# A hybrid decoder layer on one core: two feature groups interleaved in a written order, one more seven-product block, a last bank in two halves

## The chip, the cores and the metric

The kernel runs on one core of a Trainium2 chip. The metric is the device time of one execution in microseconds; a comparison takes the median of several. The engines are TensorE (PE, its weight loads PEld), VectorE (DVE), ScalarE (ACT), GpSimd (POOL) and SyncE (SP), which here issues the DMAs.

## The reference

One decoder layer for 256 tokens of width 2048, in fp32. What matters here is the first stage, the input projection, and the last, the layer norm of the output:

```python
def reference(x, mem, w_in, ...):
    proj = x @ w_in[l]
    q_m, k_m, v_m, o_m, i_m, f_m, q_a, k_a, v_a = split_columns(proj, IN_SPLITS)
    y_m = mlstm_mixer(q_m, k_m, v_m, o_m, i_m, f_m, conv_w[l], conv_b[l], gate_b[l], mh_g[l])
    y_a = dilated_attention(q_a, k_a, v_a, rel_bias)
    y = jnp.concatenate([y_m, y_a], axis=-1) @ w_out[l]
    x = layer_norm(DEEPNORM_ALPHA * x + y, ln_g[l, 0], ln_b[l, 0])
    y = memory_cross_attention(x, mem, xq[l], xk[l], xv[l], xo[l])
    x = layer_norm(DEEPNORM_ALPHA * x + y, ln_g[l, 1], ln_b[l, 1])
    y = swiglu_ffn(x, w1[l], w3[l], w2[l])
    x = layer_norm(DEEPNORM_ALPHA * x + y, ln_g[l, 2], ln_b[l, 2])

def mlstm_mixer(...):          # forget gates: log_sigmoid, cumulative sum, running maximum
    b = jnp.cumsum(log_f, axis=-1)
    m_row = jnp.maximum(inter, d_log.max(-1))
    ...

def dilated_pattern(q, k, v, rel_bias, window, dil):   # a bias table by distance, one row per head
    s = jnp.einsum('bhrnqd,bhrnkd->bhrnqk', qb, kc) * (dh ** -0.5) + bias[:, None, None]
    ...
```

## The kernel before

**Products.** Every fp32 product is made of parts: an operand is split into an upper part (a cast by ScalarE, name ending in h, L139 or L144) and a lower part (the rest, a subtraction on VectorE, name ending in l, L140 or L145), and upper × upper, upper × lower and lower × upper are summed in a bank of PSUM. x lies in eight pairs of k tiles (xT0 to xT7, L186 and L211), each 256 KB.

**Groups.** A *feature group* (i0 to i7) makes 512 columns of the query and key projections with the columns as rows of the result: eight tiles, each a k tile pair of weights, 128x1024, in 16 matmuls (eight pairs of one with 512 columns and one with 256) into four banks b0 to b3. A *row group* (v0, v1, v2 for the value columns) makes a 256 x 1024 result in four banks, named P2, P3, Q4 and E. Its plan (PLAN_V, L49) lists eight blocks of two k tiles each. A plain number is a block of 24 matmuls of 512 columns; a number in parentheses is a block by seven products (Strassen's scheme with fewer additions), 21 matmuls. For these, VectorE makes sums of the weights (L529, L537, L541), and the x of that block must have been mixed: `mix_again` (L182) adds the parts of x (L186), forms four sums of 128x128 (L175 to L178) and splits them again (ScalarE, then VectorE L140) into xTm.

**Order.** From the list `mix` on, the order of TensorE, VectorE and ScalarE is written by hand: `Stream(4)` (L407) goes through its tiles in the order in which they were added, makes the parts of the tile that is four ahead behind the products of the tile at hand (`upper` casts, `lower` subtracts), and hangs other work on a tile number at one of five places (0 ahead of the first products, 1 and 2 behind the first and second half, 3 ahead of the lower part, 4 behind it). Weights pass through 3 raw buffers (tag w, 1 MB each) and 5 buffers each for upper and lower parts. PSUM has a pool of five banks (`bank`) and one of three (`sbank`).

**The head.** i0 and i1 are made by `gemm_features` (L618) and `features` (L636) before the list begins: i0 whole, then i1 whole, in an order that the scheduler chooses. i0 loads x as it goes. The bias table (`bias_table`, L680) follows in the program: a small product pb of the one-hot table with rel_bias, a row in DRAM (line), a fetch of it broadcast over partitions (rows), and sixteen DMAs that cut it into the slots tb. Then come the constants of the convolution and gates (cw, gb, gw) and the mixes of x for j = 2, 4, 6. The list starts with v0, then i2, i3, the heads of the attention (scores sc, exponentials, `weigh` L739, and `turn` L747, which transposes on TensorE into pt), and the gates (`Gates`, L777): products, logarithms, a shift by a DMA (v0r, L812), the scans of sum and running maximum (L816 to L824, `maxima`), columns and exponents.

**The end.** The last row group is w2b1, with the products for its last eight k tiles and the second 128 rows kept back behind the list (`behind`, `kept`, LAG2 = 8). The loop at the end takes these products bank by bank, adds each to z (L1001), takes statistics (L1059), and then `finish` (L1070) scales the four pieces of z by mean and gain (L1077), then all four by the deviation (L1080), and four DMAs of 256 KB write them.

## Time and profile before

| | |
|---|---|
| median of 3 runs | 1525.39 us (1524.21 to 1526.31) |
| the profiled execution | 1525.3 us, span 1523.5 us |
| granted TensorE clock, mean | 0.998 |
| busy: PE, DVE, ACT | 1507.6, 1322.4, 832.9 us |
| DMA | 301.90 MB, 198 GB/s mean |

The span is the time from the first to the last instruction. Matmuls overlap: a matmul of 512 columns shows 0.39 us, but the next starts 0.23 us behind it, so stretches of TensorE are measured from start to start. In a timeline, x4 behind a row stands for four like instructions under one start. Where a row ends in brackets, its engine was idle before it for that long, and what stands behind the arrow ended the idle time.

### The profile page before, as it was taken

To read this page: it belongs to the slowest core of one execution; us is meant where nothing else is said; L and a number is where in the kernel's file an instruction comes from. 1 tells how busy PE (TensorE), PEld (TensorE's weight loads), DVE (VectorE), ACT (ScalarE), POOL (GpSimd) and SP (SyncE) were. 2 spreads that over 40 slices of the span, in tenths; PEclk is the share of its full clock that TensorE was granted. 3 is DMA by queue.
4 is the path that set the end of the run, shared out by engine and by line. 5 is a ranking of instruction groups with operands and counts; after the bars stand their busy time and mean duration, and the time that the engine had idled before them with its cause. 6 is when DMAs were issued, how large, how long until landed. Compare 5 with 4: busy or idle time off the path is not lost.

```text
span 1523.5 us, 19428 instructions
## 1 busy us (share of the span) xinstructions
PE 1507.6 (99%) x7340; PEld 1263.0 (83%) x7340; DVE 1322.4 (87%) x1756; ACT 832.9 (55%) x1089; POOL 8.9 (1%) x18
## 2 busy tenths in 40 slices
PE   9999999999999999999999999999999999999997
PEld 7888888888888888889888888888888888888885
DVE  7676699989999898777798889999998899998898
ACT  5455555545554456645556556556555555555551
POOL 0000000000000000000000000000000000000000
PEclk9999999999999999999999999999999999999999
DMA  8665446655656456454455465665565656666652
GB/s 306 227 231 187 165 157 224 219 196 208 202 213 221 166 196 218 166 204 156 155 181 201 161 214 194 194 208 182 196 228 180 216 194 198 198 201 222 235 194 111
DMA packets 82475, 301.90 MB, mean 198 GB/s; under 512 B 7133, under 2 KB 9422, under 8 KB 58318
## 3 DMA queue, kind: packets, MB, share of 16 engines
...
q8 instruction: 57, 0.93, 0.3%
...
## 4 chain that ended last, share of the span: by engine, by line
PE 95%; DVE 2%; issue 1%; DMA 1%; ACT 1%; SPq 0%; DVEq 0%; ACTq 0%
PE w2a0P L481 2%; PE w2a1P L481 2%; PE w2b1P L481 2%; PE w2b0P L481 2%; PE f8P L481 2%; PE f4P L481 2%; PE f10P L481 2%; PE f6P L481 2%; PE wo0P L481 2%; PE f14P L481 2%; PE f20P L481 2%; PE f18P L481 2%; PE f16P L481 2%; PE v1P L481 2%; PE f12P L481 2%; PE wo1P L481 2%
## 5 line engine op out<-in xcount | busy, mean ns | idle before, releaser
L144 ACT CAST w2a1h<-w2a1w 128x1024 fp32r<-128x1024 f32 (+1 forms) x24 | 22.7, 963 | 18.4 <-PE w2a1E L481 10.0
L145 DVE TENSOR_TENSOR w2a1l<-w2a1w,w2a1h 128x1024 fp32r<-128x1024 f32 (+1 forms) x24 | 25.8, 1107 | 3.0 <-ACT w2a1h L144 3.0
L144 ACT CAST w2a0h<-w2a0w 128x1024 fp32r<-128x1024 f32 (+1 forms) x24 | 22.5, 962 | 10.6 <-PE w2a0E L481 5.9
L145 DVE TENSOR_TENSOR v0l<-v0w,v0h 128x1024 fp32r<-128x1024 f32 (+1 forms) x16 | 17.7, 1121 | 11.3 <-ACT v0h L144 11.3
L481 PE MATMUL w2a0P<-w2a0h,hT 128*128 128x512 f32 x76 | 26.7, 392 | 0.0
L481 PE MATMUL w2a1P<-w2a1h,hT 128*128 128x512 f32 x76 | 26.5, 389 | 0.0
L145 DVE TENSOR_TENSOR w2a0l<-w2a0w,w2a0h 128x1024 fp32r<-128x1024 f32 (+1 forms) x24 | 26.0, 1106 | 0.4 <-ACT w2a0h L144 0.3
L144 ACT CAST w2b0h<-w2b0w 128x1024 fp32r<-128x1024 f32 (+1 forms) x20 | 19.5, 989 | 12.2 <-PE w2b0E L481 5.2
L145 DVE TENSOR_TENSOR w2b0l<-w2b0w,w2b0h 128x1024 fp32r<-128x1024 f32 (+1 forms) x20 | 22.2, 1137 | 3.9 <-ACT w2b0h L144 3.9
L145 DVE TENSOR_TENSOR xo0l<-xo0w,xo0h 128x1024 fp32r<-128x1024 f32 (+1 forms) x16 | 18.2, 1155 | 8.4 <-ACT xo0h L144 8.4
L294 PE MATMUL f0b<-f0h,x 128*128 128x512 f32 x64 | 25.4, 397 | 0.0
L295 PE MATMUL f0b<-f0l,x 128*128 128x512 f32 x64 | 25.1, 391 | 0.2 <-DVE f0l L1529 0.2
L144 ACT CAST w2b1h<-w2b1w 128x1024 fp32r<-128x1024 f32 (+1 forms) x20 | 18.7, 986 | 10.7 <-PE w2b0E L481 5.4
L603 PE MATMUL i2b<-xT,i2h 128*128 128x512 f32 x64 | 23.5, 408 | 0.5 <-DVE xTr L1159 0.5
L481 PE MATMUL w2b0P<-w2b0h,hT 128*128 128x512 f32 x68 | 23.9, 392 | 0.0
L144 ACT CAST v0h<-v0w 128x1024 fp32r<-128x1024 f32 (+1 forms) x16 | 15.3, 971 | 15.4 <-PE v0E L481 6.0
L144 ACT CAST f12h<-f12w 128x1024 fp32r<-128x1024 f32 (+1 forms) x16 | 15.3, 973 | 14.7 <-PE f12E L481 6.8
L603 PE MATMUL xq0b<-x,xq0h 128*128 128x512 f32 x64 | 23.1, 404 | 0.0
L603 PE MATMUL i3b<-xT,i3h 128*128 128x512 f32 x64 | 23.1, 404 | 0.0
L603 PE MATMUL i5b<-xT,i5h 128*128 128x512 f32 x64 | 23.1, 403 | 0.0
L603 PE MATMUL i4b<-xT,i4h 128*128 128x512 f32 x64 | 23.1, 403 | 0.0
L603 PE MATMUL i7b<-xT,i7h 128*128 128x512 f32 x64 | 23.1, 402 | 0.0
...
## 6 DMA issues: line engine op xcount, KB each, us to landing
...
```

The costliest lines, as they stand in the source:

```text
L144: SC.copy(hi, src)
L145: return lambda: V.tensor_tensor(out=lo, in0=src, in1=as_f32(hi), op=ALU.subtract)
L294: T.matmul(banks[m][c], xh, wh[:, cs], start=n == 0, stop=False)
L295: T.matmul(banks[m][c], xh, wl[:, cs], start=False, stop=False)
L481: T.matmul(self.of[to], lhsT, rhs, start=to not in self.begun, stop=end)
L603: T.matmul(b, wh[:, cs], self.op.both(kt), start=kt == 0, stop=end, skip_group_check=True)
```

## The change

- i0 and i1 become feature groups of the list. Their first two tiles alternate (i0 0, i1 0, i0 1, i1 1), then i0's tiles 2 to 7, then i1's. i0's first six k tiles and i1's first four are loaded each by a DMA of its own (512 KB) instead of two together (1 MB), the first one still in two halves of 256 KB. In the first tile of each group the products with upper parts precede, in each half of the weights, those with lower parts. Bank b0 of i1 comes from the pool of five, b1 to b3 from the pool of three.
- rel_bias, one-hot table and gate constants are fetched four tiles before i0's last; the mixes of x, now for j = 2, 4, 6 and 1, hang on the tiles 3 and 1 before i0's last, one behind it, and 5 before it; the table is made three tiles behind i0's last tile, in a bank of the pool of five.
- v0's plan has a fourth seven-product block and another order: 0, 3, (2), (4), 5, (6), (1), 7.
- The gates' maxima, columns and exponents come one tile later.
- At the end, bank E's products of the last three kept k tiles (CUT = 3) are made in halves of 256 columns, the second half into a bank E2 of its own. Adds and statistics follow by halves. The scalings by mean and deviation alternate, each piece's DMA follows at once, and the last piece is scaled and written in two halves. z's second 128 rows have their statistics in halves of 256 throughout this norm.

SP, from i0's second pair of weights on, before; xTraw is x, i0w and i1w are weights, rb, cw, gb and gw the constants:

```order
L277 DMA i0w_159<-in_w_qk 128x2048
L217 DMA xTraw_181<-in_xT 128x512
L217 DMA xTraw_206<-in_xT 128x512
L277 DMA i0w_211<-in_w_qk 128x2048
L217 DMA xTraw_233<-in_xT 128x512
L217 DMA xTraw_258<-in_xT 128x512
L217 DMA xTraw_285<-in_xT 128x512
L682 DMA rb<-in_rel_bias 32x8
L683 DMA rb<-in_one 1x8
L1135 DMA cw<-in_conv 128x80
L1137 DMA gb<-in_gate_b 8x1
L277 DMA i0w_263<-in_w_qk 128x2048
```

and after (xTd is a slot used first for the one-hot table, then for the last x):

```order
L217 DMA xTraw_190<-in_xT 128x512
L609 DMA i0w_164<-in_w_qk 128x1024
L217 DMA xTraw_216<-in_xT 128x512
L217 DMA xTraw_243<-in_xT 128x512
L217 DMA xTraw_269<-in_xT 128x512
L675 DMA rb<-in_rel_bias 32x8
L676 DMA rb<-in_one 1x8
L678 DMA xTd_282<-in_onehot 33x511
L1143 DMA cw<-in_conv 128x80
L1144 DMA gb<-in_gate_b 8x1
L1145 DMA gw<-in_w_gate 128x128
L609 DMA i0w_221<-in_w_qk 128x1024 x2
```

The small fetches, which stood ahead of i0's last pair only, stand ahead of its last two pairs, one of them in two loads; before these rows, SP now also issues two loads of i1 (rows not shown).

VectorE before, at i0's last two k tiles (i0l are lower parts of weights, xT of x; xTr is a mix being made):

```order
L177 TENSOR_TENSOR xTr_545<-xTr_545 128x128
L140 TENSOR_TENSOR xT_260<-xTraw_258,xT_260 128x2x256
L140 TENSOR_TENSOR xT_287<-xTraw_285,xT_287 128x2x256
L178 TENSOR_TENSOR xTr_545<-xTr_545 128x128
L186 TENSOR_TENSOR xTr_554<-xT_260 128x512
L140 TENSOR_TENSOR i0l_266<-i0w_263,i0h_265 128x1024
L175 TENSOR_TENSOR xTr_554<-xTr_554 128x128
L176 TENSOR_TENSOR xTr_554<-xTr_554 128x128
L140 TENSOR_TENSOR i0l_291<-i0w_263,i0h_290 128x1024
```

and after (xTm is the mixed x):

```order
L145 TENSOR_TENSOR i0l_276<-i0w_274,i0h_275 128x1024
L186 TENSOR_TENSOR xTr_280<-xT_126 128x512
L175 TENSOR_TENSOR xTr_280<-xTr_280 128x128
L176 TENSOR_TENSOR xTr_280<-xTr_280 128x128
L177 TENSOR_TENSOR xTr_280<-xTr_280 128x128
L178 TENSOR_TENSOR xTr_280<-xTr_280 128x128
L140 TENSOR_TENSOR xTm_287<-xTr_280,xTm_287 128x512
L140 TENSOR_TENSOR xT_315<-xTd_282,xT_315 128x2x256
L145 TENSOR_TENSOR i0l_319<-i0w_274,i0h_318 128x1024
```

Before, a mix was spread between other work; now the mix of x1, from L186 to its lower part (L140), and the last x stand in one piece between the lower parts of i0's k tiles 6 and 7.

VectorE before, at the end of i2 (v0r are the gates' rows, g and ast the softmax of a head, i3l lower parts):

```order
L145 TENSOR_TENSOR i3l_1090<-i3w_1087,i3h_1089 128x1024
L816 SCALAR_TENSOR_TENSOR xTr_563<-v0r_873,g_1029 4x256
L817 TENSOR_TENSOR xTr_563<-v0r_873,xTr_563 4x256
L818 SCALAR_TENSOR_TENSOR i0r_316<-xTr_563,g_1029 4x256
L824 TENSOR_TENSOR i0r_316<-xTr_563,i0r_316 4x256
L145 TENSOR_TENSOR i3l_1116<-i3w_1087,i3h_1115 128x1024
L741 RECIPROCAL ast_1093<-ast_1093 128x2
L743 TENSOR_SCALAR g_1030<-g_1030,ast_1093 128x256
L743 TENSOR_SCALAR g_1030<-g_1030,ast_1093 128x128
```

and after:

```order
L145 TENSOR_TENSOR i3l_1110<-i3w_1108,i3h_1109 128x1024
L145 TENSOR_TENSOR i3l_1137<-i3w_1108,i3h_1136 128x1024
L736 RECIPROCAL ast_1114<-ast_1114 128x2
L738 TENSOR_SCALAR g_1051<-g_1051,ast_1114 128x256
L738 TENSOR_SCALAR g_1051<-g_1051,ast_1114 128x128
L811 SCALAR_TENSOR_TENSOR tb_524<-v0r_894,g_1050 4x256
L812 TENSOR_TENSOR tb_524<-v0r_894,tb_524 4x256
L813 SCALAR_TENSOR_TENSOR xTd_459<-tb_524,g_1050 4x256
L819 TENSOR_TENSOR xTd_459<-tb_524,xTd_459 4x256
L145 TENSOR_TENSOR i3l_1161<-i3w_1159,i3h_1160 128x1024
```

The softmax (reciprocal and scaling, L741 and L743 before, L736 and L738 after) and the second lower part of i3 now precede the scans (L816 to L824 before, L811 to L819 after).

The diff, cut to what the prediction speaks of:

```diff
-MIXED_X = (2, 4, 6)
-PLAN_V = [[0, 1, (2,), 3, (4,), 5, (6,), 7]] * 3
+MIXED_X, MIX_X, BOTH, TABLE = (2, 4, 6, 1), (-3, -1, 1, -5), 2, 3
+PLAN_V = [[0, 3, (2,), (4,), 5, (6,), (1,), 7]] + [[0, 1, (2,), 3, (4,), 5, (6,), 7]] * 2
...
-        def __init__(self, stream, op, src, name, load=None, last=False):
-            self.name, self.rows, self.banks, self.t = name, [], [], {}
+        def __init__(self, stream, op, src, name, load=None, last=False, alone=0, own=4):
+            self.name, self.rows, self.banks, self.t, self.stream = name, [], [], {}, stream
             self.op, self.src, self.load, self.last, self.w = op, src, load, last, {}
+            self.alone, self.own = alone, own
             self.begin = len(stream.tiles)
-            for n in range(KT // 2):
-                parts = []
-                stream.tile(
-                    lambda n=n, parts=parts: self.prepare(n, parts), lambda n=n, parts=parts: self.products(n, parts)
-                )
-            self.end = len(stream.tiles) - 1
-            for j in range(2):
-                for c in range(2):
-                    stream.at(self.end, 2, self.evacuate, j, c)
+            if not alone:
+                for n in range(KT // 2):
+                    self.lay(n)
+
+        def lay(self, n):
+            parts = []
+            self.end = self.stream.tile(lambda: self.prepare(n, parts), lambda: self.products(n, parts))
+            if n == KT // 2 - 1:
+                for j in range(2):
+                    for c in range(2):
+                        self.stream.at(self.end, 2, self.evacuate, j, c)
 
         def prepare(self, n, parts):
             if self.load:
                 self.load(n)
-            if n % 2 == 0:
-                self.w[n // 2] = wp.tile([P, 2, W], F32, tag="w", name=f"{self.name}w{n // 2}", bufs=RAW)
-                nc.sync.dma_start(out=self.w[n // 2], in_=self.src[n // 2])
+            b, i = divmod(n, 2)
+            if i == 0:
+                self.w[b] = wp.tile([P, 2, W], F32, tag="w", name=f"{self.name}w{b}", bufs=RAW)
             parts += [wp.tile([P, W], F32R, tag=f"w{x}", name=f"{self.name}{x}{n}") for x in "hl"]
-            return upper_part(*parts, self.w[n // 2][:, n % 2])
+            w = self.w[b][:, i]
+            if self.alone and self.load and n == 0:
+                halves = [slice(c * 512, (c + 1) * 512) for c in range(2)]
+                for cs in halves:
+                    nc.sync.dma_start(out=w[:, cs], in_=self.src[b][:, i, cs])
+                for cs in halves:
+                    split(*(x[:, cs] for x in parts), w[:, cs])
+                return lambda: None
+            if n < self.alone:
+                nc.sync.dma_start(out=w, in_=self.src[b][:, i])
+            elif i == 0:
+                nc.sync.dma_start(out=self.w[b], in_=self.src[b])
+            return upper_part(*parts, w)
 
...
+    def bias_fetch():
         rb = const.tile([BUCKETS + 1, AH], F32, tag="rb", name="rb")
         nc.sync.dma_start(out=rb[:BUCKETS], in_=A["rel_bias"])
         nc.sync.dma_start(out=rb[BUCKETS:], in_=A["one"])
-        oh_t, gs_t = slot("oh"), slot("gs")
+        oh_t = slot("oh")
+        nc.sync.dma_start(out=oh_t[: BUCKETS + 1, :U], in_=A["onehot"])
+        table["rb"], table["oh"] = rb, oh_t
+
+    def bias_table():
+        rb, oh_t, gs_t = table["rb"], table["oh"], slot("gs")
         oh, gs = oh_t[: BUCKETS + 1, :U], gs_t[:AH, :U]
-        nc.sync.dma_start(out=oh, in_=A["onehot"])
-        pb = sbank("pb")
+        pb = bank("pb")
...
-                (0, 0, self.products), (1, 3, self.logs), (2, 4, self.shift), (4, 3, self.maxima),
-                (6, 0, self.columns),
+                (0, 0, self.products), (1, 3, self.logs), (2, 4, self.shift), (5, 3, self.maxima),
+                (7, 0, self.columns),
             ):
                 mix.at(t + dt, where, f)
             for h in range(MH):
-                mix.at(t + 8 + h, 3, self.exponents, h)
+                mix.at(t + 9 + h, 3, self.exponents, h)
...
+        def stats(self, m, c, halves=range(2)):
+            if m not in self.fine:
+                V.bn_stats(out=self.st[m][:, c], in_=z[m][c])
+                return
+            for i in halves:
+                V.bn_stats(out=self.st[m][:, 2 * c + i], in_=z[m][c][:, i * 256 : (i + 1) * 256])
...
+    i0 = FeatureGroup(mix, xT, A["w_qk"][0], "i0", load_x, alone=6)
+    i1 = FeatureGroup(mix, xT, A["w_qk"][1], "i1", alone=4, own=1)
+    for n in range(BOTH):
+        i0.lay(n)
+        i1.lay(n)
+    for group in (i0, i1):
+        for n in range(BOTH, KT // 2):
+            group.lay(n)
+    for t, j in zip(MIX_X, MIXED_X):
+        mix.at(i0.end + t, 4, xT.mix_again, j)
+    mix.at(i0.end - 4, 0, bias_fetch)
+    mix.at(i0.end - 4, 0, fetch_constants)
+    mix.at(i0.end + 1, 3, gate_weights)
+    mix.at(i0.end + TABLE, 2, bias_table)
     v0 = rows_group(0, PLAN_V[0], va)
     i2, i3 = features_group(2), features_group(3)
-    heads(0, lambda j: (qk0[j], qk0[2 + j]), 0, [i2.begin + ATT + 4 * h for h in range(4)])
...
+    def last_step(ln, scale, c, n):
+
+        for i in range(n):
+            cs = slice(i * 512 // n, (i + 1) * 512 // n)
+            t = z[1][c][:, cs]
+            V.scalar_tensor_tensor(out=t, in0=t, scalar=scale, in1=ln.b[c][:, cs], op0=ALU.mult, op1=ALU.add)
+            nc.sync.dma_start(out=A["out"][1, c][:, cs], in_=t)
+
+    for c in range(2):
+        add(0, 1, banks, 1.0, (c,))
+        ln.stats(0, 2 + c)
+    ln.finish(0)
+    for c in range(4):
+        nc.sync.dma_start(out=A["out"][0, c], in_=z[0][c])
+    for f in final.behind:
+        f(0)
+    add(1, 1, banks, 1.0, (0,))
+    ln.stats(1, 2)
+
+    final.of["E2"] = sbank("w2b1E2")
+    for f in final.behind[:-CUT]:
+        f(1)
+    for i in range(2):
+        cs = slice(i * 256, (i + 1) * 256)
+        for f in final.behind[-CUT:]:
+            f(1, cs)
+        t = z[1][3][:, cs]
+        for x in ("E", "E2")[: 1 + i]:
+            V.tensor_tensor(out=t, in0=t, in1=final.of[x][:, cs], op=ALU.add)
+        ln.stats(1, 3, (i,))
+    mean, scale = ln.scales(1)
+    t = z[1]
+    for c in range(4):
+        V.scalar_tensor_tensor(out=t[c], in0=t[c], scalar=mean, in1=ln.g[c], op0=ALU.subtract, op1=ALU.mult)
+        if c:
+            last_step(ln, scale, c - 1, 1)
+    last_step(ln, scale, 3, 2)
```

## Rows read from the trace of the kernel before

**Rows 1.** The page: busy time, share of the span and instructions of each engine.

```profile
PE 1507.6 (99%) x7340; PEld 1263.0 (83%) x7340; DVE 1322.4 (87%) x1756; ACT 832.9 (55%) x1089; POOL 8.9 (1%) x18
```

**Rows 2.** TensorE's waits: line, what for; us in total, times, longest.

```profile
PE i0b L628 <- ACT i0h L139: 1.4, 2, 1.1
PE pt L749 <- DVE g L743: 0.8, 1, 0.8
PE i2b L603 <- DVE xTr L1159: 0.5, 1, 0.5
```

**Rows 3.** Timeline of TensorE, head: start, duration, what [idle before <- releaser].

```profile
5.51 1.20 PE L628 MATMUL i0b<-xT,i0h 128*128 128x512 f32 x4 [0.27 <-ACT i0h L139]
9.78 1.20 PE L628 MATMUL i0b<-xT,i0h 128*128 128x512 f32 x4 [1.09 <-ACT i0h L139]
...
49.73 0.40 PE L628 MATMUL i1b<-xT,i1h 128*128 128x512 f32 x1
52.50 0.40 PE L628 MATMUL i1b<-xT,i1h 128*128 128x512 f32 x1
```

**Rows 4.** Windows: busy us (instructions) of PE, PEld, DVE, ACT, POOL, clock, DMA.

```profile
10.00:20.00 10.00, 9.58 (x51) 7.60 (x51) 9.86 (x17) 7.37 (x11) 0.00 (x0) 1.00 0.97 366
20.00:30.00 10.00, 10.00 (x59) 8.75 (x59) 10.00 (x18) 6.09 (x8) 0.00 (x0) 1.00 0.82 309
40.00:50.00 10.00, 10.00 (x60) 8.77 (x59) 6.62 (x6) 4.83 (x5) 0.00 (x0) 1.00 0.78 274
```

**Rows 5.** Timeline of SP: issue of two DMAs.

```profile
11.90 0.28 SPq L683 DMA_DIRECT2D rb<-in_one  x1
...
81.55 0.36 SPq L229 DMA_DIRECT2D v0w<-in_w_v  x1
```

**Rows 6.** Timeline of ScalarE: casts of i0's weights.

```profile
8.68 1.04 ACT L139 CAST i0h<-i0w 128x1024 fp32r<-128x1024 f32 x1 [1.03 <-DMA i0w<-in_w_qk]
...
11.91 2.00 ACT L139 CAST i0h<-i0w 128x1024 fp32r<-128x1024 f32 x2 [1.66 <-DMA i0w<-in_w_qk]
...
20.91 2.00 ACT L139 CAST i0h<-i0w 128x1024 fp32r<-128x1024 f32 x2 [1.60 <-DMA i0w<-in_w_qk]
```

**Rows 7.** Timeline of TensorE: start of v0, and eight spacings.

```profile
53.99 0.50 PE L481 MATMUL v0P<-v0h,xT 128*128 128x512 f32 x1 [0.53 <-DVE i0r L644]
...
59.11 0.39 PE L481 MATMUL v0P<-v0h,xT 128*128 128x512 f32 x1
...
60.92 0.39 PE L481 MATMUL v0E<-v0h,xT 128*128 128x512 f32 x1
```

**Rows 8.** Timeline of VectorE: first and last operation of a seven-product block.

```profile
79.53 1.22 DVE L529 TENSOR_TENSOR v0t<-v0w 128x1024 f32<-128x1024 f32 x1
...
84.89 1.22 DVE L145 TENSOR_TENSOR v0l<-v0s,v0h 128x1024 fp32r<-128x1024 f32 x1
```

**Rows 9.** Timeline of ScalarE: the cast of v0's last weights.

```profile
87.56 2.00 ACT L144 CAST v0h<-v0w 128x1024 fp32r<-128x1024 f32 x2 [2.71 <-DMA v0w<-in_w_v]
```

**Rows 10.** Timeline of TensorE: first and third pair of i2.

```profile
96.90 0.47 PE L603 MATMUL i2b<-xT,i2h 128*128 128x512 f32 x1
...
98.53 0.50 PE L603 MATMUL i2b<-xT,i2h 128*128 128x512 f32 x1
```

**Rows 11.** Timeline of VectorE: the gates' first scan.

```profile
119.94 0.68 DVE L816 TENSOR_TENSOR_SCAN xTr<-v0r,g 4x256 f32<-4x256 f32 x1 [2.45 <-DMA v0r<-v0r]
```

**Rows 12.** Chain that ended last, tail: start, us, what.

```profile
1513.34 0.70 DVE z L1001
...
1514.06 0.71 DVE l2st L1059
...
1514.79 0.27 DVE l2mv L1064
```

**Rows 13.** Groups of VectorE by form: statistics of 256 columns: busy, mean ns.

```profile
L942 DVE BATCH_NORM_STATS2 mst<-mh 128x6 f32<-128x256 f32 x8 | 3.0, 418 | 0.0
```

**Rows 14.** DMA issues of the tail: KB each, median us to landing.

```profile
out<-z SPq DMA_DIRECT2D x8, 256.0 KB, 2.0
```

123 lines of the change are left out of this document (45 added, 78 removed).

## The prediction

> **What bounds the kernel now.** I read the page first: TensorE is busy for 1507.6 us, 99% of the 1523.5 us span, and VectorE for 87% [rows 1]. So time can come from three places only: fewer products, waits of TensorE, and the ends of the span where it has nothing to do. The list of TensorE's waits comes next [rows 2]: the first feature group i0 waits 1.4 us for ScalarE's casts, one transposition (pt) waits 0.8 us and group i2 waits 0.5 us, all for work that the change moves. These sums are idle time only; what a stall costs is read from start to start in the timeline. In the head the first product starts at 5.51 and the second tile at 9.78, where TensorE waited 1.09 us for the cast of i0's second k tile; at the other end eight product pairs, one tile, take 52.50 − 49.73 = 2.77 us [rows 3]. Sixteen tiles of i0 and i1 are 44.3 us, and the first pair of the next group would start at 52.50 + 0.35 = 52.85. Hence 52.85 − 5.51 − 44.3 = 3.0 us were lost in the two groups, almost all of it in i0's first tiles. The windows say why: from 10 to 20 us the DMA engines are 0.97 busy and move 366 GB/s, and VectorE is busy for 9.86 of 10 us, then all of the next 10; from 40 to 50 it is down to 6.62 and TensorE is never short [rows 4]. The head waits for bytes, and next to that for VectorE.
>
> The sum below is made against the profiled run, 1525.3 us with a span of 1523.5 us. It lies 0.1 us below the median of the three runs, so I use it for the median too.
>
> **The first two groups side by side.** Today every tile of i0 needs a new 256 KB of x and, for each k tile, 512 KB of weights. With i1's first two k tiles put between, the second tile uses x that is already there. Its price: 1 MB of i1 is now fetched ahead of i0's later weights.
> - Second tile. Today its 512 KB are behind the second x and land just before the cast at 8.68 [rows 6]; now they are ahead of that x, 256 KB less. At the 366 GB/s of [rows 4] 256 KB are 0.7 us, so the cast starts near 7.9 and the tile near 9.0 instead of 9.78. TensorE is through the first tile at 5.51 + 2.77 + 0.3 (the wait for the second half of the first weights, which stays) = 8.6. Lost: 0.3 + 0.4, and 0.25 more for the lower part, which VectorE makes behind the cast. The third and fourth tiles bring one weight load each and one x between them, so they should find their data.
> - i0's last weights. SP issues a small DMA at 11.90 [rows 5], just as i0's second pair has landed for the cast at 11.91 [rows 6]: it waits for a landing, so the queue has a limited number in flight, and the six small fetches (bias, gate weights) now stand ahead of i0's k tiles 4 to 7, which is where the changed order costs. Today the last 1 MB of i0 lands just before the cast at 20.91 [rows 6]. One more MB ahead of it is 1.05 / 366 = 2.9 us: 23.7 us; with one or two more for the small fetches, and the one-hot table that today is fetched much later, 25.4. k tile 6 is the ninth tile and is due at 5.51 + 8 × 2.77 + 0.95 = 28.6, its cast (half of the 2.00 us for two, [rows 6]) and lower part (1.22, [rows 8]) in time. But VectorE has in its order, between the lower parts of k tiles 6 and 7, the whole first mix (two operations of 128x512 at about 0.7 and four of 128x128, an estimate of 0.27 each: 256 columns are 0.418 [rows 13], 512 are 0.71 [rows 12], so half of the 256 is 0.15 less), a cast of ScalarE inside it and the last x. From 25.4: cast 1.0, lower part 1.2, mix 0.7 + 1.1, cast 0.5, two of 0.65, lower part 1.1, that is 32.3. Tile 7 is due at 31.4. So I book a new wait of 0.9 there; from 23.7 it would be none.
> - Later tiles. A mix comes every second tile: two lower parts (2 × 1.15), a mix with its waits (some 2.9) are 5.2 us against 2 × 2.77 = 5.54 of TensorE. It fits, barely; I book 0.15.
> Lost after: 0.3 + 0.4 + 0.25 + 0.9 + 0.15 = 2.0, against 3.0: 1.0 gained, between 0 (a wait of 1.9 at tile 7) and 1.9.
>
> **The start of v0.** Its third product waited for the evacuation of i1 and started at 53.99, where spacing asks for some 53.3: 0.7 with what follows it [rows 7]. Now i1 ends in three banks of the small pool and one of the large, and v0 begins in banks that i0 left ten tiles earlier. Gain 0.7 to 0.8; I take 0.8. The bias table's product (pb) stands on TensorE in i1 as it did in v0, with the same operands: its time only moves, which I book at nothing.
>
> **One more seven-product block in v0.** Three products of 512 columns fewer. Eight spacings are 60.92 − 59.11 = 1.81 [rows 7], so each is 0.226 and the gain 0.68. It costs VectorE: a seven runs from 79.53 to the end of the lower part at 84.89 + 1.22, about 6.5 us [rows 8], against 21 × 0.226 = 4.75 us of TensorE. Two of these in a row fall 3.5 us behind; the plain blocks on either side (2.3 us of lower parts in 24 × 0.226 = 5.4) give 3.1 back each, and in [rows 4] VectorE has a third of its time free just ahead of this region. The cover is four tiles of work ahead. If it were gone, up to 1.7 us per seven would show, which is where the lower end of the range comes from. I book nothing. The new mix of x for it lies in the head and is booked above.
>
> **From v0 to i2.** The first pair of i2 starts at 96.90, the third at 98.53 [rows 10], where two pairs are 2 × 0.35 = 0.7: 0.9 lost, of which 0.5 is plain waiting [rows 2] for the sums that clear v0's banks. They are late because ScalarE waited 2.71 us for v0's last weights [rows 9], and these because their DMA was issued at 81.55 [rows 5], behind the sixteen table DMAs. Now the table is made in i1, some 17 us earlier, and two loads of v0 instead of one stand behind its DMAs. SP passes them long before. The sums then start earlier by up to the 2.5 us that VectorE idled, but four other steps and i2's lower parts stand ahead of them. Between 0 (the wait only moves) and 1.2 (the next pairs late by a third as well), I take 0.8.
>
> **Gates.** VectorE waits 2.45 us for the shifting DMA at 119.94 [rows 11], and the softmax that pt waits for is queued behind it. With the scans one tile (2.77 us) later, the softmax is ahead of them and the DMA has landed. TensorE's 0.78 [rows 2] costs 0.93 from start to start. Behind the scans now stand only the third lower part of i3, four tiles ahead, and the columns, moved by one tile as well. I take 0.93, between 0.5 and 0.95.
>
> **The tail.** TensorE pays nothing for eighteen products of 256 columns in place of nine of 512 but a few fixed costs, 0.05. VectorE after the last product: today add, statistics and aggregate start at 1513.34, 1514.06 and 1514.79 [rows 12]. Now the first half is ready 9 × 0.113 = 1.0 us before the end, at 1512.3, and three adds and two statistics of 256 columns follow; nearest row, 0.418 each [rows 13], 0.44 with the gap: 1512.3 + 2.2 = 1514.5. Gain 0.3. The last scaling is halved: the last DMA begins on 128 KB, and of the 2.0 us of a 256 KB one [rows 14] some 0.3 are bytes at 366 GB/s; against it stands one more fixed cost of VectorE, 0.15. Together 0.45, between 0.2 and 0.7. The halved statistics earlier in the group cost VectorE 2 × 0.418 for 0.71 [rows 12, 13], some 0.14 each; they run beside kept tiles, and I book 0.05 for all of them.
>
> **Sum.** 1.0 + 0.8 + 0.68 + 0.8 + 0.93 + 0.45 − 0.1 = 4.6 us: 1525.3 − 4.6 = 1520.7.
>
> **Rivals.**
> *The waits only move.* The sums of v0 come as late as before since VectorE makes i2's lower parts first, and the scans, now a tile later, hold up the columns instead. Then 0.8 + 0.93 fall away: gain 2.9, 1522.4, within 0.2% by a hair. For it: VectorE is 87% busy, and both waits are for VectorE. Against it: both have a DMA behind them in the rows, and the change passes these.
> *The bytes come late.* In the head 7.3 MB (x, i0 and the first MB of i1) must land before k tile 6. From about 2 us at 366 GB/s that is done at 22; if the six small transfers take places among the few in flight and cut the rate to 270 GB/s, it is 29.2, and tile 7, 6.9 us of cast, mix and lower parts later, is ready at 36.1, 4.7 us late where 0.9 is booked: gain 0.8, 1524.5. For it: the queue is bound by what is in flight [rows 5], and 309 GB/s is all that the next window shows [rows 4]. Against: that window is one in which SP waited for buffers.
> *Slower.* The same place with small loads as such: eight loads of 512 KB take the place of four of 1 MB. Slower by 3.05 us needs tile 7 to be 4.6 + 3.05 = 7.65 us later than booked: weights landed at 31.4 + 0.9 + 7.65 − 6.9 = 33.1, or a rate below 7.3 / (33.1 − 2) = 235 GB/s. Then 1528.4 or more. Against it stand 366 GB/s in a stretch that is half 256 KB loads of x, since several are in flight. The Trainium skill, "DMA: Bandwidth & Descriptors", section "Bandwidth", asks for 1 MB or more per DMA, and its "Anatomy of one DMA" gives about 2 us fixed plus bytes at 436 GB/s, by which (an estimate) one 512 KB load after the other would run at some 160 GB/s and this rival would hold with a time over 1535; the 366 GB/s show that the fixed part overlaps here.
> *Not what it says.* If the table's product, one tile earlier or later, met its own late fetch, TensorE would wait in i1; its fetch goes out ahead of i0's fifth k tile and is used some 20 us later, so I give this nothing.
>
> **How the numbers follow.** Forecast as summed: 0.72. Waits only move: 0.12. Bytes late: 0.11. Slower: 0.05. The upper ends of the terms together (1.9 + 0.8 + 0.68 + 1.2 + 0.95 + 0.7) are 6.2, 1519.1; the forecast's own range is 1519.1 to 1522.3. A measurement of this kernel tells 0.2%, 3.05 us, from no change: faster means below 1522.3. The first rival lies at that line; I count a fifth of it and a tenth of the second to faster: 0.75. Same: 0.20. Slower: 0.05. For 8 in 10 the range takes in the first rival and the easier part of the second, and 0.3 below the forecast's own for the scatter of a median: 1518.8 to 1523.3.
>
> **What would show it.** Right: the second tile near 9.0 and v0's first product near 52.9 with pb (about 1 us) already done; no wait of v0 for the evacuation; pt and i2 gone from TensorE's list; 21 products in each of four blocks of v0; aggregate about 1.2 us after the last product ends. Wrong: a wait of i0 or i1 for weights at 25 to 35 us, waits of v0 for VectorE's lower parts in the two adjoining sevens, or i2 still waiting for the sums.

## The result and the profile after

The changed kernel takes 1528.17 us (median of 19 runs, 1526.53 to 1530.40); the kernel before, run beside it, 1525.66 us (19 runs, 1524.21 to 1527.16). The ratio is 1.0016, with a 95% interval of 1.0010 to 1.0023. The forecast was 1520.7 us, in a range that ended at 1523.3: wrong in size and in sign. By the prediction's own bound of 0.2% the change made no difference that counts, but the interval lies above 1: 2.5 us were lost where 4.6 were to be gained.

The profiled execution of after took 1527.06 us with a span of 1525.2, against 1525.3 and 1523.5 before. It is one of the shorter ones of after, 1.1 us below the median, so that part of the loss stands in no trace of after. The page's line of busy times, which answers to [rows 1]:

```profile
PE 1508.5 (99%) x7346; PEld 1264.7 (83%) x7346; DVE 1330.4 (87%) x1774; ACT 835.5 (55%) x1092; POOL 8.9 (1%) x18
```

TensorE's waits, which answer to [rows 2] (us in total, times, longest):

```profile
PE i0b L624 <- ACT i0h L139: 2.6, 1, 2.6
...
PE i2b L624 <- DVE i1r L1158: 1.0, 1, 1.0
PE i0b L626 <- DVE i0l L145: 0.5, 1, 0.5
```

The wait of pt is gone. i0 has one wait of 2.6 us, i2 waits twice as long as before, and i0 waits for VectorE at its last k tile, where before it did so at its third (0.4 us, not in [rows 2]). Cut at the first product of a stage, the span divides like this (us; all starts are those of TensorE's instructions, "end" is the end of the span):

| stretch | before | after | difference |
|---|---|---|---|
| start to i0's first product | 5.51 | 5.29 | −0.22 |
| i0 and i1, to v0's first (after holds pb, 1.05) | 47.34 | 52.02 | +4.68 |
| v0, to i2's first (before holds pb) | 44.05 | 42.19 | −1.86 |
| i2, to i3's first | 32.22 | 31.71 | −0.51 |
| i3 to the last group, unchanged | 1331.60 | 1330.96 | −0.64 |
| last group, to its last product | 52.19 | 52.53 | +0.34 |
| last product to the end | 10.61 | 10.55 | −0.06 |

The unchanged stretch took between 1330.8 and 1331.9 us in fourteen profiles, so a sum of stages carries about 1 us of scatter, which the prediction had no row for. The loss sits in the second line. The next view is ScalarE's timeline in the head of after, the counterpart of [rows 6]:

```profile
9.26 0.62 ACT L139 CAST i0h<-i0w 128x512 fp32r<-128x512 f32 x1 [4.02 <-DMA i0w<-in_w_qk]
```

The second half of i0's first weights, 256 KB, was cast at 9.26; it had been issued at about 1.65, as in before. TensorE's timeline in the same place, the counterpart of [rows 3]:

```profile
9.93 2.08 PE L624 MATMUL i0b<-xT,i0h 128*128 128x512 f32 x4 [2.60 <-ACT i0h L139]
...
12.65 1.24 PE L624 MATMUL i1b<-xT,i1h 128*128 128x512 f32 x4
```

After 2.6 us without work, the four pairs from 9.93 took 2.72 us, where a half tile takes 1.39. The windows of after say why (columns as in [rows 4]):

```profile
4.00:6.00 2.00, 1.95 (x4) 0.62 (x3) 1.39 (x2) 0.81 (x2) 0.00 (x0) 1.00 0.74 152
6.00:8.00 2.00, 1.33 (x8) 1.00 (x6) 0.00 (x0) 0.00 (x0) 0.00 (x0) 1.00 0.85 246
8.00:10.00 2.00, 0.07 (x1) 0.07 (x1) 0.09 (x1) 0.62 (x1) 0.00 (x0) 0.89 1.01 406
10.00:12.00 2.00, 2.00 (x5) 1.62 (x6) 0.97 (x2) 1.45 (x2) 0.00 (x0) 0.50 1.04 418
...
16.00:18.00 2.00, 2.00 (x13) 1.72 (x13) 1.87 (x3) 1.35 (x2) 0.00 (x0) 1.00 0.57 193
18.00:20.00 2.00, 2.00 (x13) 1.76 (x12) 1.55 (x3) 1.57 (x2) 0.00 (x0) 1.00 0.28 91
```

And the same first windows of before:

```profile
4.00:6.00 2.00, 1.73 (x4) 0.45 (x3) 1.20 (x2) 0.72 (x2) 0.00 (x0) 1.00 0.91 224
6.00:8.00 2.00, 2.00 (x12) 1.67 (x11) 1.18 (x3) 1.24 (x2) 0.00 (x0) 1.00 1.05 386
8.00:10.00 2.00, 0.91 (x6) 0.66 (x6) 0.61 (x2) 1.32 (x2) 0.00 (x0) 1.00 1.05 434
```

Between 4 and 8 us the DMA engines moved 152 and 246 GB/s where they had moved 224 and 386. From 8 to 16 us the rates are alike; from 16 to 20 they fall to 193 and 91, where before had 209 and 407. The granted clock fell to 0.50, the 1.2 GHz level, while products ran, after the 2.6 us of idle.

Per tile (from one tile's first product to the next one's), with 2.77 as the prediction's measure:

```
before  4.27  3.24  3.54  then 2.66 to 3.01, mean 2.79
after   7.37  2.92  then 2.80 to 2.83 in ten tiles, 3.60 at the tile from 35.37, 3.82 with pb, 2.96 behind it, 3.10 the last
```

So once the first tile is through, TensorE waits only once more in the two groups. But that tile costs 4.6 us instead of 1.5, and the tile from 35.37 another 0.8. A tile in the steady part takes 2.83 rather than 2.79. That is not the change's doing: the head of before, in "the head undone", has 2.77 to 2.84 as well, after's order in the runs "xq" and "x early" has 2.77, and "three sevens" goes from 2.83 to 2.77 and back within the head, all at a granted clock of 1.00. What makes it 2.77 or 2.83 no run shows.

### The profile page after: what moved, and what is told of

The parts are those of the page before. It is cut to its first block, busy times and chain, and to the rows that moved or that the text cites. A ratio compares the mean times of both kernels' runs of the same rounds, so it can differ in the third digit from the quotient of the medians.

```text
span 1525.2 us, 19461 instructions
## 1 busy us (share of the span) xinstructions
PE 1508.5 (99%) x7346; PEld 1264.7 (83%) x7346; DVE 1330.4 (87%) x1774; ACT 835.5 (55%) x1092; POOL 8.9 (1%) x18
## 4 chain that ended last, share of the span: by engine, by line
PE 91%; DMA 3%; DVE 3%; issue 1%; ACT 1%; SPq 0%; DVEq 0%; ACTq 0%
PE w2a0P L482 2%; PE w2a1P L482 2%; PE w2b1P L482 2%; PE w2b0P L482 2%; PE f18P L482 2%; PE f4P L482 2%; PE f6P L482 2%; PE f16P L482 2%; PE wo0P L482 2%; PE f20P L482 2%; PE f14P L482 2%; PE f10P L482 2%; PE f8P L482 2%; PE v1P L482 2%; PE f12P L482 2%; PE wo1P L482 2%
## 5 line engine op out<-in xcount | busy, mean ns | idle before, releaser
L624 PE MATMUL i0b<-xT,i0h 128*128 128x512 f32 x64 | 23.6, 424 | 2.6 <-ACT i0h L139 2.6
L294 PE MATMUL f0b<-f0h,x 128*128 128x512 f32 x64 | 25.4, 397 | 0.0
L624 PE MATMUL i6b<-xT,i6h 128*128 128x512 f32 x64 | 23.2, 404 | 0.0
```

The lines of the kernel that those rows point to most:

```text
L294: T.matmul(banks[m][c], xh, wh[:, cs], start=n == 0, stop=False)
L624: T.matmul(b, w, self.op.both(kt), start=kt == 0, stop=end, skip_group_check=True)
```

## The experiments

Two theories stood against each other at first. A: the loss is the head's first tile, where i1's weights, as the fourth DMA, hold up the second half of i0's. B: it is VectorE, which a fourth mix and a fourth seven-product block overload. Times are medians; each ratio is against runs of before on the same chip. Each kernel has one profile, and a profile is one execution: that of "tail undone" is 1.3 us above its median, that of "i0 first" 1.4 below.

**The head undone.** Everything of the change but the first two groups, which run as before: one after the other, 1 MB loads, table in v0.

```diff
-    for n in range(BOTH):
-        i0.lay(n)
-        i1.lay(n)
...
+    qk0 = in_features(0, load_x) + in_features(1)
+    tb = bias_table()
```

> The change with i0 and i1 made as before it (one after the other, 1 MB loads, order of the scheduler, table and constants as before); v0's fourth seven, the gates and the tail stay as changed. Theory A (the loss is in the head: the second half of i0's first weights lands at 9.2 instead of 6.3 us, TensorE waits 2.6 us and then runs at the lower clock): the first tile is on time again, v0 starts about 2.5 us earlier counted without pb, and the time is about 1525.7 us. Theory B (the loss is in v0, where two sevens in a row and late last weights hold VectorE up): it stays near 1528.2.

1525.06 us (11 runs); ratio 0.9999, 0.9990 to 1.0007. Three microseconds against after come back: the head is where the time went. But the rest of the change, which this kernel has, then gains nothing that the interval shows. The waits of its TensorE:

```profile
PE i0b L650 <- ACT i0h L139: 2.0, 3, 1.0
...
PE i2b L624 <- DVE xTr L1189: 0.2, 1, 0.2
```

and ScalarE's cast of that second half:

```profile
6.55 0.62 ACT L139 CAST i0h<-i0w 128x512 fp32r<-128x512 f32 x1 [0.85 <-DMA i0w<-in_w_qk]
```

**Three sevens only**, without the x1 mix.

```diff
-MIXED_X, MIX_X, BOTH, TABLE = (2, 4, 6, 1), (-3, -1, 1, -5), 2, 3
-PLAN_V = [[0, 3, (2,), (4,), 5, (6,), (1,), 7]] + [[0, 1, (2,), 3, (4,), 5, (6,), 7]] * 2
+MIXED_X, MIX_X, BOTH, TABLE = (2, 4, 6), (-3, -1, 1), 2, 3
+PLAN_V = [[0, 1, (2,), 3, (4,), 5, (6,), 7]] * 3
```

> The change with three sevens in v0 in the order of before, and without the mix of x1; all else as changed. Theory A (loss in the head by late bytes): 0.7 us of products come back, some 0.75 us of waits in v0 and up to 0.8 us of the wait at i0's last k tile go; the time is 1527.0 to 1528.3 us, and the first tile still waits over 2 us for its second half. Theory B (loss in v0): 1524 to 1525.5 us, with the sums of v0 early enough for i2.

1525.44 us (11 runs); 0.9995, 0.9986 to 1.0003: 2.7 us below after. Theory A had said 1527.0 to 1528.3; the time lies in the range of theory B, though i2 still waits 0.9 us for the sums, which B said would come early enough. In its profile the second half is late again, but by less, and the clock stayed at 1.00; ScalarE's timeline, and TensorE's waits:

```profile
8.40 0.62 ACT L139 CAST i0h<-i0w 128x512 fp32r<-128x512 f32 x1 [3.04 <-DMA i0w<-in_w_qk]
```

```profile
PE i0b L624 <- ACT i0h L139: 1.6, 2, 1.4
```

and the wait at i0's last k tile is gone, which was x1's mix. v0 begins at 55.08 us, 2.2 sooner than in after. v0 to i2 took 42.50 us here and 42.19 in after: so the fourth seven, which should save 0.68, saved 0.31 there. In the profiles of "tail undone" and "xq", which have it too, v0 took 43.54 and 43.81, with waits of 1.1 and 1.4 us for VectorE's lower parts: there it lost over 1 us.

**The tail undone.**

```diff
-        norm["l2"] = Norm(2, "l2", (1,))
+        norm["l2"] = Norm(2, "l2")
...
+                for f in final.behind:
+                    f(c)
+            add(m, 1, banks, 1.0, (c,))
+            ln.stats(m, 2 + c)
```

> The change with the end as before: bank E whole, statistics of 512 columns, scalings one after the other, eight output DMAs of 256 KB. Theory A (the halves brought nothing since the last DMA is not shorter for its 128 KB and one more fixed cost stands on VectorE): 1528.2 us within 0.4. The forecast's step (0.45 us gained by the halves): 1528.6. Theory C (the halves cost): below 1527.7.

1528.84 us (11 runs); 1.0016, 1.0007 to 1.0025, after's own ratio. From the last group's first product to the end it took 52.19 + 10.90 = 63.09 us, after 52.53 + 10.55 = 63.08. The halves are worth nothing: this stretch takes 62.8 to 63.2 us in the eleven profiles with them and 62.8 to 63.1 in the three without. (The median alone, 0.7 us above after's, would fit the forecast's step; the interval doesn't tell.) Its head had a wait of 2.8 us at the same place, with the clock at 1.00 throughout, so the wait does not always bring the lower clock.

**i0's two first k tiles before i1's**, otherwise all of the change. Now the fourth DMA of the program is x's second 256 KB, as in before, and not i1's weights.

```diff
         i0.lay(n)
+    for n in range(BOTH):
         i1.lay(n)
```

> The change with its first four tiles in the order i0 0, i0 1, i1 0, i1 1, so that x1 and i0's second k tile are fetched ahead of i1's first. Theory A (i1's first 512 KB right behind i0's halves delay the second half): it lands near 6.3 again, the first tile ends near 8.4, the second tile waits until about 9.8 as before the change, the clock stays up, and the time is 1525 to 1526 us. Rival (the small loads or the scheduled order as such bring the lag of four DMA engines): the second half still lands past 8.5 and the time stays near 1528.

1525.64 us (ten runs, 1523.36 to 1527.48; an eleventh of 3914.67 us is left out); 1.0000, 0.9991 to 1.0009. The cast of the second half:

```profile
6.31 0.62 ACT L139 CAST i0h<-i0w 128x512 fp32r<-128x512 f32 x1 [0.45 <-DMA i0w<-in_w_qk]
```

No lag; its first two tiles take 3.65 and 3.95 us and all later ones 2.81 to 2.83, but for those around pb, without the wait at i0's last k tiles. 2.5 us go with an order of loads. But two things differ in that order: the fourth DMA, and, which the edit doesn't name, the weights of i0's k tiles 4 and 5, which SP here issues ahead of three of the six small fetches and in after behind them all. SP here:

```profile
13.71 1.57 SPq L609 DMA_DIRECT2D i0w<-in_w_qk  x2
15.61 0.33 SPq L1143 DMA_DIRECT2D cw<-in_conv  x1
```

**What delays the second half: the addresses?** i1's weights are read from another input, xq, so that i1's features are not those of the reference.

```diff
-    i1 = FeatureGroup(mix, xT, A["w_qk"][1], "i1", alone=4, own=1)
+    i1 = FeatureGroup(mix, xT, A["xq"][0], "i1", alone=4, own=1)
```

> The change, but i1's weights are read from another input of the same shape (xq's first group), so what i1 computes is not the reference's; orders and sizes of the DMAs are as changed. If the lag of some DMA engines comes from the addresses of i1's weights, which lie right behind i0's, the second half of i0's first weights lands near 6.3 us and the wait of the first tile goes. If it comes from the place and size of the load (512 KB in rows of 4 KB as the fourth DMA), the last of the 16 pieces still lands past 8.2 us and TensorE waits 1.4 to 2.8 us.

1529.29 us, one run. The lag stays, with a wait of TensorE of 1.2 us, so it isn't bound to where w_qk[1] lies:

```profile
8.38 0.62 ACT L139 CAST i0h<-i0w 128x512 fp32r<-128x512 f32 x1 [3.01 <-DMA i0w<-in_w_qk]
```

**Or the size of the fourth DMA?** The order of the last but one, with i0's own second k tile, 512 KB, ahead of x.

```diff
-            if self.load:
+            if self.load and not (self.alone and n == 1):
...
+                if self.load and n == 1:
+                    self.load(n)
...
```

> Tiles in the order i0 0, i0 1, i1 0, i1 1 as in the run lay, but x1 is fetched behind i0's second k tile and not ahead of it, so the fourth DMA is 512 KB in rows of 4 KB again, this time of i0. If place and size of the load make the lag, the second half of the first weights lands past 8 us as in the change; if only i1's region or i1's being a second group does, it lands near 6.3 as in lay.

1525.53 us, one run. Both halves are cast by 6.45:

```profile
5.18 1.27 ACT L139 CAST i0h<-i0w 128x512 fp32r<-128x512 f32 x2 [1.11 <-DMA i0w<-in_w_qk]
```

A 512 KB load in the fourth place does not delay the one ahead of it, when it is i0's own. The time says nothing of the head: i0 and i1 took 51.64 us, nearly as long as in after. The first tile took 5.62, since its first eleven products followed each other at 0.43 us and more (a half of that is usual), at a granted clock of 1.00 in the rows; the second took 5.47, with waits of 0.9 and 0.8 and a clock of 0.50 from 12.8 us. v0 and i2 then took 2.2 us less than in after.

**x fetched early, tiles in after's order.**

```diff
+            elif self.alone and n == 0:
+                load_x(1)
```

> The change with its own order of tiles, but x1 is fetched ahead of i1's first k tile, so the fourth DMA is 256 KB in rows of 2 KB as before the change. If place and size of the fourth load make the lag, the second half lands at 6.2 to 6.6 us, the first tile ends near 8.5, i1's first tile starts near 9.7, the clock stays up and the time is 1526.0 us or less, as in lay; if it is i1's region, the lag stays and the time is near 1528.

1527.16 us (11 runs); 1.0007, 0.9998 to 1.0015, above the 1526.0 that the sentence allows. The second half is cast at 6.16: the lag goes with the fourth DMA, not with the order of the products. But i1's first weights come one place later and it waits for them, and i0's last two k tiles cost 1.7 us by their waits: the weights of k tiles 4 to 7 stand behind the small fetches as in after. ScalarE's timeline, and TensorE's waits:

```profile
6.16 0.62 ACT L139 CAST i0h<-i0w 128x512 fp32r<-128x512 f32 x1 [0.21 <-DMA i0w<-in_w_qk]
```

```profile
PE i1b L626 <- ACT i1h L144: 0.9, 1, 0.9
PE i0b L628 <- DVE i0l L145: 0.8, 1, 0.8
```

**The table, earlier.** In the head of "i0 first", its product two tiles earlier.

```diff
-MIXED_X, MIX_X, BOTH, TABLE = (2, 4, 6, 1), (-3, -1, 1, -5), 2, 3
+MIXED_X, MIX_X, BOTH, TABLE = (2, 4, 6, 1), (-3, -1, 1, -5), 2, 1
...
```

> The run lay with the bias table made two tiles earlier (one tile behind i0's last), so that SP passes line, rows and the sixteen table DMAs ahead of v0's fifth load and none of v0's loads stands behind them. If the wait of i2 for the sums of v0 (1.1 us in lay) comes from v0's last loads standing behind the table, it falls to 0.3 or less, and the time is about 1 us below lay's, 1525.0. If it comes from VectorE's own work (two sevens in a row, four early steps and i2's lower parts ahead of the sums), it stays and the time is 1526.

1527.86 us (11 runs); 1.0017, 1.0008 to 1.0026. i2's wait fell to 0.4, but the product, now ahead of i0's evacuation, stopped TensorE itself:

```profile
42.27 1.02 PE L685 MATMUL pb<-xTd,rb 33*8 33x511 f32 x2 [3.25 <-DVE xTd L636]
```

**The table, later.** In the same head, its way to DRAM starts four tiles into v0, so that all of v0's loads go ahead of it.

```diff
...
+    mix.at(v0.begin + 4, 4, table_rows)
...
```

> The run lay with the table's row held back: pb is made as before, but a copy of one element four tiles into v0 releases the row's DMA, so that all of v0's loads go out ahead of the sixteen table DMAs. If i2's wait for v0's sums (1.1 us in lay) comes from the two loads that stood behind the table, it falls to 0.3 us or less, v0 takes 0.8 to 1.2 us less up to i2's second tile, and the time is 1.0 us below lay, 1525.0. If VectorE's own order makes it, the wait stays above 0.8 us and the time is lay's, 1526.

1530.12 us (7 runs); 1.0035, 1.0024 to 1.0046. No block of v0 waits any more, but the loads behind the table do: the casts of i2's weights wait 6.07 us for them, and v0's sums stand on VectorE behind i2's lower parts. So the scores and i2 wait for sums (the slot tb, in these rows, holds such sums). TensorE's waits, and SP's timeline:

```profile
PE sc L724 <- DVE tb L1033: 2.9, 1, 2.9
PE i2b L624 <- DVE tb L1165: 1.5, 1, 1.5
```

```profile
80.27 7.32 SPq L705 DMA_DIRECT2D tb<-rows  x12
87.70 10.29 SPq L611 DMA_DIRECT2D i2w<-in_w_qk  x4
```

The same with three sevens (the constants of "Three sevens only"):

> The run lay_l4 with three sevens in v0 in the order of before, and without the mix of x1. The forecast's step says that the fourth seven is worth its three products, so this is 0.7 us slower than lay_l4. If the fourth seven only moves the end of v0 to VectorE, v0's products and the wait of i2 together take as long as in lay_l4 and the two are equal within 0.3 us.

1528.40 us (11 runs); 1.0018, 1.0009 to 1.0027. It doesn't decide its question: i2 waited 3.7 us for v0's sums, which stood behind i2's late weights as before, and the block's worth is lost in that.

**The gates alone**, in the kernel before.

```diff
-                (0, 0, self.products), (1, 3, self.logs), (2, 4, self.shift), (4, 3, self.maxima),
-                (6, 0, self.columns),
+                (0, 0, self.products), (1, 3, self.logs), (2, 4, self.shift), (5, 3, self.maxima),
+                (7, 0, self.columns),
...
-                mix.at(t + 8 + h, 3, self.exponents, h)
+                mix.at(t + 9 + h, 3, self.exponents, h)
```

> The kernel before with the gates' maxima, columns and exponents one tile later, and nothing else of the change. If the step on the gates was right, pt is gone from TensorE's list and the time is 0.9 us below before, 1524.7 to 1525.0; if the wait only moves, pgate or a later product waits instead and the time is that of before.

1524.42 us (11 runs), before 1525.89 (23 runs); 0.9995, 0.9986 to 1.0004: the lowest median measured, a little below what was expected, though the interval still takes in 1. i2 to i3 takes 30.72 us instead of 32.22. The scan, which waited 2.45 us in [rows 11], waits for nothing:

```profile
120.58 0.67 DVE L816 TENSOR_TENSOR_SCAN xTr<-v0r,g 4x256 f32<-4x256 f32 x1
```

**The fourth seven, in a sound head**: the head of before, with the rest of the change, and three sevens.

```diff
-MIXED_X, MIX_X, BOTH, TABLE = (2, 4, 6, 1), (-3, -1, 1, -5), 2, 3
-PLAN_V = [[0, 3, (2,), (4,), 5, (6,), (1,), 7]] + [[0, 1, (2,), 3, (4,), 5, (6,), 7]] * 2
+MIXED_X, MIX_X, BOTH, TABLE = (2, 4, 6), (-3, -1, 1), 2, 3
+PLAN_V = [[0, 1, (2,), 3, (4,), 5, (6,), 7]] * 3
...
```

> This is the run with the head of before (head_back: the first two groups one after the other, 1 MB loads, table in v0; the gates later, the tail in halves) with three seven-product blocks in v0 instead of four and without the mix of x that the fourth needs. Theory A: the fourth seven is worth its products wherever VectorE is given time for the extra mix, and in the changed kernel it cost some 2 us only because its mix fell into the same stretch as i0's last tiles and the adjoining blocks followed a starved head. Then here v0 takes 0.68 us more from its first product to i2's first than the 43.32 us of head_back (44.0), its three sevens start without a wait, and the median is 0.3 to 1.0 us above head_back's 1525.06, if the scatter lets that be seen. Theory B: a fourth seven is paid back by VectorE in any head. Then the stretch is 43.3 or less, by waits that head_back has in v0 and this kernel has not, and the time is equal to head_back's or below it. The span from i3's first product to the end is the same in both, within 0.3 us.

1524.68 us (ten runs, 1523.36 to 1526.59; an eleventh of 8683 us is left out); 1.0001, 0.9992 to 1.0011. v0's first to i2's first took 44.09 us, with four sevens 43.32: 0.77 for the 0.68 that the block promises, with the same wait of 0.5 for the evacuation at v0's start in both and no other in v0. And i2 waits longer here:

```profile
PE i2b L624 <- DVE xTr L1189: 0.7, 1, 0.7
```

So in a head that VectorE has finished in time the block is worth its products, by one profile of each. The times can't show it: the ratios, 0.9999 and 1.0001, differ by 0.3 us that way, inside both intervals (the medians themselves were taken on two chips, on which before took 1525.78 and 1524.88). The stretch behind i3 differed by 0.7 us between the two profiles, not the 0.3 expected of it, so a verdict on 0.7 us rests on the stage, not on the time.

## Why the prediction was wrong, and where it was right

**The first two groups: the step that failed.** 2.0 us were booked as lost in i0 and i1; by the same measure, without pb, 52.02 − 1.05 − 44.3 = 6.7 came. Two terms of it were wrong: the 0.3 for the second half of the first weights, and the landing of i0's last weights. The second is the one that v0's start followed.

**The first half tile.** The prediction booked a wait of 0.3 for the second half of the first weights, "which stays". It reckoned with each load's place behind others, never with what a load does to those ahead of it. With i1's weights as the fourth DMA the second half was cast at 9.26, 8.40, 9.43 and 8.38 (after, three sevens, tail undone, xq); with x's second part, or i0's own second k tile, at 6.31 to 6.55 (before, head undone, i0 first) and by 6.16 (x early; the 512 KB one as well), and its last piece landed by 6.9 in the five other profiles. That is shown by four kernels against ten, with one profile each. A DMA comes in 16 pieces, and the trace marks each one's landing; for the second half of the first weights these are

```
before     4.6 4.6 4.6 4.7 4.7 4.9 5.0 5.0 5.3 5.3 5.5 5.8 6.0 6.2 6.2 6.3
after      5.0 5.0 5.1 5.1 5.2 5.2 5.2 5.2 5.3 5.7 5.7 5.9 8.2 9.0 9.1 9.2
i0 first   4.4 4.6 4.7 4.8 4.8 5.0 5.1 5.1 5.5 5.6 5.6 5.7 5.9 5.9 6.3 6.3
```

In after twelve are in time and four 3 us late; in "tail undone", "three sevens" and "xq" five, seven and eight come behind 6.4 us. The cast waits for all 16. In the loads issued up to 12 us later first and last piece lie 3.3 to 3.9 us apart in after, 1.0 to 1.5 in before. The Trainium skill, "DMA: Bandwidth & Descriptors", section "Queues, rings and completion order", says that one DMA is spread over rings of up to 16 engines, each taking its descriptors in order. That the last four pieces of the later loads come as late again agrees with that, though the trace doesn't tell which engine brought a piece. Why a load of another tensor in that place makes pieces late, and i0's own of the same size does not, stays open: the addresses of w_qk[1] alone are ruled out, the size alone too. The load that does harm also fills another buffer than i0's, and no run tells tensor and buffer apart.

In after's profile the first tile cost 4.6 us where 0.7 to 0.95 were booked. Of it 2.76 is the wait, 1.33 the half tile at the lower clock, 0.5 the first half. But this is not what the whole run lost. The lower clock is no fixed price of that wait: with 2.8 us of waiting in "tail undone" it stayed at 1.00. And of after's 19 runs ten have a mean granted clock of 0.998, like before, and nine a lower one; their medians are 1528.19 and 1528.17.

**i0's last weights, k tile 7: wrong, and its 0.9 came by luck.** A wait of 0.9 behind the first mix was booked, and 0.8 came, at the same place. But the weights were booked to land at 25.4 and the lower part of k tile 7 to be done at 32.3, for a tile due at 31.4. ScalarE, TensorE, then VectorE:

```profile
28.86 1.05 ACT L144 CAST i0h<-i0w 128x1024 fp32r<-128x1024 f32 x1 [2.29 <-DMA i0w<-in_w_qk]
...
35.37 0.39 PE L624 MATMUL i0b<-xT,i0h 128*128 128x512 f32 x1
36.28 0.39 PE L626 MATMUL i0b<-xT,i0l 128*128 128x256 f32 x1 [0.52 <-DVE i0l L145]
...
29.95 1.22 DVE L145 TENSOR_TENSOR i0l<-i0w,i0h 128x1024 fp32r<-128x1024 f32 x1 [1.77 <-ACT i0h L144]
31.09 0.69 DVE L186 TENSOR_TENSOR xTr<-xT 128x512 f32<-128x512 f32 x1
...
35.00 1.23 DVE L145 TENSOR_TENSOR i0l<-i0w,i0h 128x1024 fp32r<-128x1024 f32 x1 [0.18 <-ACT i0h L144]
```

The mix stands between the two lower parts, as the prediction read from the order, and cast, mix and lower parts take 7.4 us where 6.9 were reckoned. But the weights came 3.5 us late and the lower part was done at 36.23, 3.9 late; the wait is short only because TensorE was 4 us late itself. From there on the first tile no longer matters. In the four profiles with after's order and the mix of x1 (us):

| | first tile | cast of k tile 6, ending a wait for its weights | wait at k tile 7 ends | v0's first product |
|---|---|---|---|---|
| after | 7.37 | 28.86 | 36.28 | 57.31 |
| tail undone | 6.20 | 29.51 | 36.91 | 57.92 |
| xq | 5.79 | 28.99 | 36.39 | 57.37 |
| x early, no lag | 4.00 | 27.08 | 34.48 | 55.49 |

v0 starts 21.0 us behind the wait's end, and that is 7.4 us behind the cast, whatever the first tile took. So both theories had a part: the late weights, and the mix that stands behind them. Without the mix (three sevens) v0 starts at 55.08, with the weights in time (i0 first) at 54.23:

```profile
25.07 1.05 ACT L144 CAST i0h<-i0w 128x1024 fp32r<-128x1024 f32 x1 [3.14 <-PE i0b L626]
```

Here that cast waits for TensorE to free a buffer and no longer for bytes. The weights are late because SP issues them late. In after each issue from 9.25 to 18.58 us follows the landing of an earlier load, which the lag has put off, and one small fetch after another goes out ahead of them:

```profile
13.81 0.34 SPq L675 DMA_DIRECT2D rb<-in_rel_bias  x1
...
18.58 0.35 SPq L1145 DMA_DIRECT2D gw<-in_w_gate  x1
19.26 0.85 SPq L609 DMA_DIRECT2D i0w<-in_w_qk  x2
...
20.68 0.43 SPq L611 DMA_DIRECT2D i0w<-in_w_qk  x1
```

Of the 3.5 us beyond the booked landing 1.8 go with the lag (28.86 against 27.08 in "x early"); that the rest is the price of the fetches is read from the traces, and no run moved the fetches alone. It is the rival "bytes late", at its place and nearly to the time: it put the weights at 29.2 and k tile 7 at 36.1, and its 7.3 MB by 28.8 us are 272 GB/s for its 270. The rate was not low throughout: 406 to 418 GB/s from 8 to 12 us with 512 KB loads, then 193 and 91 from 16 to 20, where "i0 first" has 346 and 367. The rule of the Trainium skill, "DMA: Bandwidth & Descriptors", section "Bandwidth", that the prediction weighed under "slower" (1 MB or more per DMA, measured there for DMAs issued from GpSimd, where SP issues here) would have given the right sign by a mechanism that these windows don't show.

**Start of v0: right.** No wait for the evacuation (0.8 booked).

**The fourth seven: "book nothing" failed in part.** Its products went (−0.68), and the blocks beside it waited 0.28 and 0.25 us plus what follows each, 0.75 in all: VectorE was busy for 5.95 of the 6 us from 86 on.

```profile
86.00:92.00 6.00, 5.80 (x25) 4.17 (x24) 5.95 (x8) 4.33 (x6) 0.00 (x0) 1.00 0.78 295
```

The cover named, four tiles of work ahead, was gone, because VectorE had idled for v0's late loads just before (next point). And the mix that it needs was booked in the head at a wait of 0.9, but holds up k tile 7 behind weights that are late already. So the block loses in this head, while in the head of before it gains 0.77. Median against median, "three sevens only" is 2.7 us below after; in the profiles v0 begins 2.2 us sooner there. A shorter first wait and an unbroken clock don't explain these: "xq" had both, with the mix, and its v0 began no sooner than after's.

**v0 to i2: wrong.** "SP passes them long before" was the step. SP's timeline of after, to set beside [rows 5]:

```profile
41.91 13.00 SPq L229 DMA_DIRECT2D v0w<-in_w_v  x3
55.17 0.29 SPq L688 DMA_DIRECT2D line<-xTd  x1
...
75.66 3.97 SPq L698 DMA_DIRECT2D tb<-rows  x8
79.74 0.84 SPq L229 DMA_DIRECT2D v0w<-in_w_v  x2
```

The product is made at 47.47, 14 us earlier than in before (61.24), but the table's first DMA is issued at 55.17: it is queued behind a load of v0 that needs a raw buffer. The 16 DMAs of the table still end just before v0's last loads, two of them now, issued at 79.74 where the last one was at 81.55. So VectorE and ScalarE wait as in [rows 9], and the sums are late:

```profile
85.50 1.23 DVE L535 TENSOR_TENSOR v0t<-v0w 128x1024 f32<-128x1024 f32 x1 [2.15 <-DMA v0w<-in_w_v]
...
85.57 1.58 ACT L144 CAST v0h<-v0w 128x512 fp32r<-128x512 f32 x2 [3.49 <-DMA v0w<-in_w_v]
...
100.32 1.28 DVE L1158 TENSOR_TENSOR i1r<-i1r,v0P 128x512 f32<-128x512 f32 x2
...
101.05 0.50 PE L624 MATMUL i2b<-xT,i2h 128*128 128x512 f32 x1 [0.97 <-DVE i1r L1158]
```

0.8 was booked as a gain; the wait doubled from [rows 2]. An earlier product (0.4 left of it, at 3.3 in pb) and a later table (0 in v0, 4.4 behind it) only move it.

**Gates: right.** pt has left the list, here and in the kernel with the gates alone, where i2 to i3 is 1.5 us shorter (0.93 booked; the rest is in part i2's own wait, 0.5 before and none there).

**Tail: the mechanism right, the size wrong.**

```profile
1514.70 0.28 PE L482 MATMUL w2b1E<-w2b1h,hT 128*128 128x256 f32 x1
...
1515.70 0.43 DVE L1062 BATCH_NORM_STATS2 l2st<-z 128x6 f32<-128x256 f32 x1
1516.16 0.37 DVE L1067 BATCH_NORM_AGGREGATE l2mv<-l2st 128x2 f32<-128x48 f32 x1
...
1520.61 1.54 DVE L1758 SCALAR_TENSOR_TENSOR z<-z,l2r,l2b 128x512 f32<-128x512 f32 x3
```

The aggregate starts 1.2 us after the last product's end, as said, 1.46 after its last start, where [rows 12] has 1.88 behind a last start at 1512.91. But with twice the records it takes 0.37 for 0.26, and the scaling has one more operation. The last DMA of 128 KB is issued 0.14 us behind VectorE's end where that of 256 KB followed in 0.03; it lands 1.89 us after its issue for 2.08, so that 0.2 of the booked 0.3 us of bytes came, and the span ends 1.07 us behind the landing for 0.88. And the last group is 0.34 longer, not 0.1: 17 spacings of 0.120 between the products of 256 columns are 2.04 against eight of 0.226, 1.81, and TensorE's weight loads waited twice some 0.2 us for VectorE's lower parts, beside which the halved statistics now stand; that these are the rest is argued, not tried apart.

Together, by the stages of the table: 4.4 us too little for the head, 0.7 for v0 with its sevens, 1.2 for i2, 0.6 for the last group and the tail, less 0.6 that the unchanged stretch happened to give, is 6.3 of the 6.4 us between 1520.7 and the profiled 1527.06. The 1.1 us from there to the median are in no trace of after; the longer k tiles 6 and 7 and the longer v0 of "tail undone" and "xq" show where it may lie.
